# Cached keys of the sample attention: four loads by quarters of partitions and a 32 by 32 block transpose on VectorE, in place of one load, four TensorE transposes and a copy

## The chip, the cores and the metric

The kernel runs on one core of one Trainium2 chip. The metric is the device time of one execution in microseconds, the median of several runs. The engines that the text speaks of are TensorE (PE; its weight loads are PEld), VectorE (DVE), ScalarE (ACT), GpSimd (POOL) and SyncE (SP), whose instruction list holds the DMA issues. The transfers themselves run on the core's 16 DMA engines.

## The reference

One step of a hybrid layer is computed for two request groups that share all weights: a prompt of 2048 tokens, and 8 sample sequences of 16 tokens each that have a cache of 1024 keys and values. The model width is 1024.

```python
h = rms_norm(x, norm_g[l])
(a_x, a_b, a_c, a_z, g_q, g_f, g_i, g_z,
 s_q, s_k, s_v, s_z, m_a, m_b, m_c) = split_cols(h @ w_in[l])
...
y_conv, conv_new = causal_conv(a_c * a_x, conv_w[l], conv_past)   # branch A
...
S_new, o_hg = hgrn_scan(S0, q_hg, log_f, k_in, v_hg)              # branch B
...
q = rms_norm(s_q.reshape(B, T, SB_HEADS, SB_DH), q_norm_g[l])     # branch C
k = rms_norm(s_k.reshape(B, T, SB_HEADS, SB_DH), k_norm_g[l])
v = s_v.reshape(B, T, SB_HEADS, SB_DH)
if past_k is None:
    o_sb = sb_prompt(q, k, v)
else:
    o_sb = sb_attend(q, concat([past_k, k]), concat([past_v, v]), P + jnp.arange(T), jnp.arange(P + T))
...
m = sigmoid(m_a) * y_a + sigmoid(m_b) * y_b + sigmoid(m_c) * y_c
return x + m @ w_out[l], conv_new, S_new, k, v
```

The change lies in the last case of branch C, the attention of the 8 sample sequences over their caches. Its scores are `z = q k / 8` per head; for each query the weights are `sigmoid(z)` times the product of `sigmoid(-z)` over all later keys, and the result is their sum over the values. There are 8 heads of 64. The cached keys lie in memory as (sequence, key, head, 64), in float32, so a key's 8 heads are a row of 512 numbers, 2 KB. For the scores the 64 numbers of a head must lie along the partitions, so the keys have to be turned.

## The kernel before, in words

**Stages.** The tokens are 17 tiles of 128, tile 0 being the samples. They go through the input projection in three groups (`GROUPS`, L39) of 5, 6 and 6 tiles; then come the rest of the prompt attention and the merge with the output projection. In each group `run_jobs` (L1317 on) walks a list of jobs. A job is one block of weights and what is done with its product: a channel job (`proj_chan`, L704 to 714) holds 24 matmuls of 128x384 for each of two chunks of three tiles (L710), a token job (`proj_tok`, L716 to 725) 72 matmuls of 128x256 for each (L721). Each product is made in three passes of a high and a low half (`PASS3`), and `split` (L173 to 176) makes the halves: ScalarE copies the high half, VectorE subtracts it for the low one.

**Weights.** In the first group weights are read from `w_in` and split, and the halves are kept in device memory (`W<-w`). In later groups `wload` (L188 to 219) reads the kept halves: mostly both in one load of 1 MB (`w<-W`, L208), every fourth time in two loads of 512 KB (`wst<-W`, L201). Weights of job i+1 are loaded when job i starts; the pool has three buffers for `w` and two for `wst`.

**Background work.** `sample_attention` (L389 on) is a generator. It is added after the first group, and between the matmuls of the jobs of group 1 `run_jobs` lets it go on, at a rate that `RATES` and the yielded costs set (L1365); what is left is drained at the group's end (L1381). All of it lies between about 560 and 1340 us of the profiled execution. A scheduler then puts each engine's instructions into an order of its own, by its own costs, so that the order in the code is not the one that runs. DMAs are issued by SP in that order; one that waits for its producer or its buffer holds up all behind it.

**The step that is changed.** The cache has 8 blocks of 128 keys for each of 8 sequences, 64 blocks in all. They are handled in 24 groups of 2 or 3 blocks. `keys(m)` (L448 to 461) handles the blocks of group m. For each block it loads 128 keys with all heads into `kc`, 128 partitions of 2 KB (L455, 256 KB); has TensorE make four transposes of 128x128 with the unit matrix `idf` into PSUM (L458); and has ScalarE copy the result to the turned keys `kt` (L459). `kc` has three buffers, `kt` two. `scores` (L470 to 491) multiplies the queries with `kt` on TensorE (L476), takes two sigmoids on ScalarE and a scan and a product on VectorE (L489, L490). `turned` (L493 to 511) turns the weights (L499) and loads the values (`vc`, L506), and `values` (L513 to 530) multiplies them (L522) and stores the rows (L529).

**Other names.** `GM<-gm` (L1177) stores a merge gate after each chunk of a gate job, `SZ<-gm` (L1185) a SiLU gate. `OX<-...` (L182) stores branch results in two halves. `mwx`, `mwp` (L1298, L1302) are loads, splits and stores of the merge weights, spread over group 1. `post_qk` (L809 to 831) handles the normed queries and keys. `xt` are tiles of activations for the next group.

Of the kernel before, what the change touches and what calls it, by code (L numbers as in the profile page):

```python
# [8 lines left out]
F32 = mybir.dt.float32  # L9
# [7 lines left out]
P = 128  # L17
# [81 lines left out]
def trunk(ctx: ExitStack, tc: tile.TileContext, x_prompt, x_sample, cache_conv, state_hgrn, cache_k, cache_v,  # L99
# [3 lines left out]
    nc = tc.nc  # L103
# [37 lines left out]
    def ps_tp(dt=F32):  # L141
        return pst[0].tile([P, 512], dt, tag="tp", name="tp")
# [19 lines left out]
    idf = const.tile([P, P], F32, name="idf")  # L162
# [226 lines left out]
    def sample_attention():  # L389

        sx = ExitStack()
        sa = sx.enter_context(tc.tile_pool(name="sa", bufs=2, side="right"))
# [52 lines left out]
        def blocks(m):  # L445
            return 2 if order[m][1] == 2 else 3

        def keys(m):  # L448

            b, sg = order[m]  # L450
            kt = sa.tile([P, 4, 384], F32, tag="kt", name="kt", bufs=2)
            for bi in range(blocks(m)):
                blk = 3 * sg + bi
                kc = sa.tile([P, 512], F32, tag="cst", name="kc", bufs=3)
                nc.sync.dma_start(kc, cache_k[0, b, blk * P:(blk + 1) * P].rearrange("t h d -> t (h d)"))  # L455
                tp = ps_tp()
                for h in range(4):
                    nc.tensor.transpose(tp[:, h * P:(h + 1) * P], kc[:, h * P:(h + 1) * P], idf)  # L458
                nc.scalar.copy(kt[:, :, bi * P:(bi + 1) * P], tp.rearrange("p (h t) -> p h t", h=4))  # L459
                yield 1.3  # L460
            held[m] = [kt]

# [69 lines left out]

        last = len(order) - 1
        yield from keys(0)
        scores(0, masked(0))
        yield 0.7
        for m in range(last + 1):
            if m < last:
                yield from keys(m + 1)
            turned(m)  # L540
            yield 2.0
            z = masked(m + 1) if m < last else None
            values(m)
            if z is not None:
                scores(m + 1, z)
            yield 2.2
        oc = sa.tile([P, 512], F32, tag="cst", name="oc", bufs=3)
        nc.sync.dma_start(oc, OCS)
        tp = ps_tp()
# [982 lines left out]
```

## Time and profile before

| | us |
|---|---|
| median of 3 runs | 2872.75 (2871.84 to 2873.47) |
| profiled execution, its own time | 2876.11 |
| its span, first to last instruction | 2873.2 |
| TensorE busy in the span | 2853.0 |
| VectorE / ScalarE / GpSimd busy | 1546.5 / 1018.7 / 331.8 |
| 64 key blocks: loads issued | 563.2 to 1119.0 |
| 64 key blocks: transposes on TensorE | 599.1 to 1138.6 |

The profile is one execution of the program. Matmuls are pipelined, so that the time of one (its "mean ns") holds an overlap with its neighbours; what a matmul adds to the path is read from the chain of waits. The windows view gives each engine's busy time in a stretch of the span, the clock granted to TensorE, the share of the 16 DMA engines in use and what they moved. A row of the waits view is: engine, tile and line that waited, what it waited for, us in total, times, longest. "To landing" is the time from a DMA's issue to the landing of its data. SPq is SP's own queue of instructions.

### The profile page before, as it was taken

How to read it: one execution, taken by the hardware profiler on the slowest of the kernel's cores; microseconds unless marked ns; L12 is line 12 of the kernel's file. 1: busy time of each engine (PE TensorE's matmuls, PEld its weight loads, DVE VectorE, ACT ScalarE, POOL GpSimd, SP SyncE). 2: the span in 40 equal slices, each digit the busy share in tenths (PEclk: the TensorE clock that was granted, in tenths of full speed). 3: DMA queues.
4: the chain of work that ended last, by engine and by line, in shares of the span. 5: the costliest groups of instructions: out<-in, count | busy, mean ns of one | idle time of the engine just before them, and what ended most of it. 6: DMA issues, size and time to landing. Idle time of an engine off the chain costs nothing.

```text
span 2873.2 us, 51723 instructions
## 1 busy us (share of the span) xinstructions
PE 2853.0 (99%) x19479; PEld 2662.3 (93%) x19479; DVE 1546.5 (54%) x3304; ACT 1018.7 (35%) x2375; POOL 331.8 (12%) x802
## 2 busy tenths in 40 slices
PE   9999999999999999999999999999999999999999
PEld 9999999999999999999999999999998888787888
DVE  5454635641344442545434747557485876867743
ACT  4333222242233332213334444434444444544420
POOL 3110000111200000001323111111010011010100
PEclk9999999999999999999999999999999999999999
DMA  8887777777678887746766454544447877878876
GB/s 306 305 276 247 231 241 244 231 243 243 212 249 266 276 265 243 243 167 192 237 215 202 146 173 136 173 139 151 144 145 238 286 234 239 266 250 266 271 250 210
DMA packets 370475, 649.76 MB, mean 226 GB/s; under 512 B 33481, under 2 KB 246306, under 8 KB 339506
## 3 DMA queue, kind: packets, MB, share of 16 engines
q1 hardware_dynamic: 369458, 644.36, 68.2%
q8 instruction: 154, 2.52, 0.4%
q0 software_dynamic: 768, 2.10, 0.2%
q14 instruction: 95, 0.78, 0.1%
HBM read 447.06 MB, written 199.27 MB: 225 GB/s over the span
## 4 chain that ended last, share of the span: by engine, by line
PE 76%; DVE 2%; DMA 2%; issue 1%; ACT 0%; POOL 0%; SPq 0%; DVEq 0%; POOLq 0%; ACTq 0%
PE acc L710 33%; PE acc L721 10%; PE acc L1440 9%; PE acc L1471 6%; PE pv L359 4%; PE tp L310 4%; PE z L330 2%; PE z L329 2%; PE z L1039 1%; PE tp L458 1%; DMA gate<-GM 1%; PE pv L522 1%; PE z L476 0%; PE hg L1086 0%; PE hg L826 0%
## 5 line engine op out<-in xcount | busy, mean ns | idle before, releaser
L710 PE MATMUL acc<-hx,w 128*128 128x384 f32 (+1 forms) x6816 | 1251.8, 333 | 0.1
L710 PEld LDWEIGHTS acc<-hx,w 128*128 128x128 f32 x6816 | 1106.5, 188 | 21.9 <-issue 15.2
L721 PE MATMUL acc<-w,hx 128*128 128x256 f32 x2544 | 328.6, 284 | 1.8 <-DVE hx L176 0.9
L342 DVE TENSOR_TENSOR_SCAN pr<-snb,carry 128x513 f32<-128x513 f32 x192 | 246.5, 1284 | 153.3 <-ACT snb L333 151.7
L721 PEld LDWEIGHTS acc<-w,hx 128*128 128x128 f32 x2544 | 310.9, 188 | 5.0 <-DVE hx L176 1.7
L311 ACT COPY aT<-tp 128x512 f32<-128x512 f32 (+2 forms) x320 | 167.6, 524 | 375.2 <-PE tp L310 361.3
L710 PE MATMUL acc<-hx,wst 128*128 128x384 f32 x1248 | 247.2, 344 | 0.0
L1440 PE MATMUL acc<-o,w 128*128 128x512 f32 (+2 forms) x1080 | 234.7, 363 | 1.8 <-DMA o<-OX 1.8
L333 ACT ACTIVATE snb<-z 128x512 f32<-128x512 f32 (+2 forms) x320 | 172.4, 539 | 144.5 <-PE z L330 140.4
L710 PEld LDWEIGHTS acc<-hx,wst 128*128 128x128 f32 x1248 | 215.4, 188 | 6.4 <-issue 3.7
L1440 PEld LDWEIGHTS acc<-o,w 128*128 128x128 f32 x1080 | 185.1, 188 | 33.8 <-issue 5.3
L347 DVE TENSOR_TENSOR sp<-sp,pr 128x512 f32<-128x512 f32 (+2 forms) x320 | 195.3, 611 | 29.2 <-POOL sp L338 3.7
L342 DVE TENSOR_TENSOR_SCAN pr<-snb,one 128x129 f32<-128x129 f32 (+3 forms) x128 | 114.4, 894 | 123.9 <-POOL snb L338 123.6
L310 PE MATMUL tp<-idf,sp 128*128 128x128 f32 x1088 | 171.3, 273 | 2.5 <-ACT aT L311 1.5
L335 ACT ACTIVATE sp<-z 128x512 f32<-128x512 f32 (+2 forms) x320 | 171.5, 536 | 0.0
L1471 PE MATMUL acc<-w,mh 128*128 128x256 f32 x816 | 161.2, 285 | 1.0 <-DVE yt L1479 0.8
L1176 ACT ACTIVATE gm<-acc 128x384 f32<-128x384 f32 (+1 forms) x144 | 68.2, 474 | 230.4 <-PE acc L710 197.5
L310 PEld LDWEIGHTS tp<-idf,sp 128*128 128x128 f32 x1088 | 131.8, 141 | 19.3 <-issue 4.4
L176 DVE TENSOR_TENSOR w<-wst,w 128x1024 fp32r<-128x1024 f32 x72 | 88.1, 1223 | 110.7 <-ACT w L175 107.9
L1471 PEld LDWEIGHTS acc<-w,mh 128*128 128x128 f32 x816 | 131.0, 188 | 7.2 <-issue 4.2
L329 PE MATMUL z<-Kt,Q 128*128 128x512 f32 (+2 forms) x320 | 128.8, 403 | 0.3 <-ACT sp L335 0.2
L359 PE MATMUL pv<-aT,Vt 128*64 128x512 f32 (+3 forms) x640 | 128.1, 535 | 0.0
(299 smaller groups left out, 3570.1 us busy)
## 6 DMA issues: line engine op xcount, KB each, us to landing
w<-W SPq DMA_DIRECT2D x168, 1024.0 KB, 6.0
W<-w SPq DMA_DIRECT2D x72, 1024.0 KB, 5.0
wst<-W SPq DMA_DIRECT2D x112, 512.0 KB, 5.1
wst<-in_w_in_dram SPq DMA_DIRECT2D x72, 512.0 KB, 5.1
GM<-gm SPq DMA_DIRECT2D x120, 192.0 KB, 3.7
W<-mwp SPq DMA_DIRECT2D x40, 512.0 KB, 4.2
Kt<-KT SPq DMA_DIRECT2D x160, 128.0 KB, 3.1
o<-OX SPq DMA_DIRECT2D x72, 256.0 KB, 4.7
```

Source lines behind the costliest of these rows:

```text
L310: nc.tensor.transpose(tp[:, j * P:(j + 1) * P], sp[:, j * P:(j + 1) * P], idf)
L311: nc.scalar.copy(aT[:, e, 0:nb, i * P:(i + 1) * P], tp[:, :w].rearrange("p (b q) -> p b q", q=P))
L329: nc.tensor.matmul(z[:, :w], Q1[:, i * P:(i + 1) * P], Kt[:, :w], start=True, stop=False)
L333: nc.scalar.activation(sn[:, 512 - w:512], z[:, :w], AF.Sigmoid, scale=-0.125)
L335: nc.scalar.activation(sp[:, :w], z[:, :w], AF.Sigmoid, scale=0.125)
L342: nc.vector.tensor_tensor_scan(pr[:, 512 - w:513][:, ::-1], s_in, s_in, one if diag else carry[e][i], ALU.mult, ALU.bypass)
L347: nc.vector.tensor_tensor(sp[:, :w], sp[:, :w], pr[:, 513 - w:513], ALU.mult)
L359: nc.tensor.matmul(pv[64 * e:64 * e + 64, c0:n], Vt[:, j, e], aT[:, e, j, c0:n], start=first and j == 0, stop=last and j == nb - 1, skip_g ...
L710: nc.tensor.matmul(acc[:, :n], w[0][a][:, k], hT[b][:, k, :n], start=k == 0 and i == 0, stop=k == KB - 1 and i == 2)
L721: nc.tensor.matmul(acc[:, :256], hT[b][:, k, ti * P:(ti + 1) * P], w[k // 4][a][:, k % 4], start=k == 0 and i == 0, stop=k == KB - 1 and i ...
L1440: nc.tensor.matmul(acc[:, :n], w[0][a][:, k, dd * P:(dd + 1) * P], box[x][b][:, k, sl], start=k == 0 and i == 0, stop=k == 3 and i == 2)
L1471: nc.tensor.matmul(acc[:, :256], box["l" if b else "h"][:, k, ti * P:(ti + 1) * P], w[k // 4][a][:, k % 4], start=k == 0 and i == 0, stop= ...
```

## The change

Only `keys(m)` is changed. `kc` becomes a tile of `[128, 4, 4, 32]`, the same bytes with the same three buffers. It is filled by four DMAs. The `a`-th of them fills partitions 32a to 32a+31: partition 32a+p gets, for each of four pairs of heads h and each of four groups c of 32 keys, the numbers 32a to 32a+31 of key 32c+p. Each DMA so moves 64 KB in 512 runs of 128 bytes. Then one `transpose` on VectorE, which turns each block of 32 by 32 in place, writes the block of `kt`. TensorE's four transposes, the PSUM tile and ScalarE's copy go. `kt` holds the same numbers as before. Lines behind the change have numbers one higher.

```diff
             for bi in range(blocks(m)):
                 blk = 3 * sg + bi
-                kc = sa.tile([P, 512], F32, tag="cst", name="kc", bufs=3)
-                nc.sync.dma_start(kc, cache_k[0, b, blk * P:(blk + 1) * P].rearrange("t h d -> t (h d)"))
-                tp = ps_tp()
-                for h in range(4):
-                    nc.tensor.transpose(tp[:, h * P:(h + 1) * P], kc[:, h * P:(h + 1) * P], idf)
-                nc.scalar.copy(kt[:, :, bi * P:(bi + 1) * P], tp.rearrange("p (h t) -> p h t", h=4))
+
+                kc = sa.tile([P, 4, 4, 32], F32, tag="cst", name="kc", bufs=3)
+                keys_ = cache_k[0, b, blk * P:(blk + 1) * P].rearrange("(c p) h d -> p c (h d)", p=32)
+                keys_ = keys_.rearrange("p c (h x) -> p h c x", x=P)
+                for a in range(4):
+                    nc.sync.dma_start(kc[32 * a:32 * a + 32], keys_[:, :, :, 32 * a:32 * a + 32])
+                nc.vector.transpose(kt[:, :, bi * P:(bi + 1) * P].rearrange("p h (c q) -> p h c q", q=32), kc)
                 yield 1.3
```

The scheduler orders all engines anew. Two places of the resulting order are shown.

The first is SP's list in the middle of group 1, around the load of a kept weight, `W_3188`. Before, it stands between two key loads; behind it come stores of branch results (`OX`), merge weights (`W_9533`, `mwx`) and the next weights (`wst`):

```order
L455 DMA kc<-in_cache_k_dram 128x512
L208 DMA w<-W_3188 128x2048
L455 DMA kc<-in_cache_k_dram 128x512
L506 DMA vc<-in_cache_v_dram 128x512
L455 DMA kc<-in_cache_k_dram 128x512
L182 DMA OX<-sg 128x384
L182 DMA OX<-y 128x384
L1298 DMA W_9533<-mwp 256x1x512
L1302 DMA mwx<-in_w_branch_dram 128x2x256
L201 DMA wst<-W_3264 128x1024 x2
L182 DMA OX<-sg 128x384
L182 DMA OX<-y 128x384
```

Directly behind these, still before the change, come the first two gate stores (`GM<-gm`):

```order
L506 DMA vc<-in_cache_v_dram 128x512 x2
L509 DMA vnew<-VV 16x512
L1177 DMA GM<-gm 128x384
L182 DMA OX<-oh 128x256
L1298 DMA W_9533<-mwp 256x1x512
L182 DMA OX<-ob 128x256
L1302 DMA mwx<-in_w_branch_dram 128x2x256
L208 DMA w<-W_3327 128x2048
L1177 DMA GM<-gm 128x384
```

After the change the same weight stands here in SP's list (a key block is now four rows in one, `x4`; `oh` and `ob` are the two halves of a branch result):

```order
L182 DMA OX<-sg 128x384
L182 DMA OX<-y 128x384
L208 DMA w<-W_3083 128x2048
L1299 DMA W_9497<-mwp 256x1x512
L1303 DMA mwx<-in_w_branch_dram 128x2x256
L182 DMA OX<-oh 128x256
L182 DMA OX<-ob 128x256
L1178 DMA GM<-gm 128x384
L459 DMA kc<-in_cache_k_dram 32x16x32 x4
L1178 DMA GM<-gm 128x384
L208 DMA w<-W_3188 128x2048
```

So the load of `W_3188` has moved from ahead of both pairs of `OX` stores to directly behind the second gate store.

The second place is TensorE's list in the same part of group 1. Before, two blocks of key transposes (`tp<-idf,kc`) stand among the matmuls of channel jobs, ahead of a transpose of attention weights (`tp<-idf,sps`):

```order
L710 MATMUL acc<-hx,w 128x384 x18
L1112 MATMUL tp<-idf,on 128x128 x2
L710 MATMUL acc<-hx,w 128x384 x6
L458 MATMUL tp<-idf,kc 128x128 x4
L710 MATMUL acc<-hx,w 128x384 x6
L710 MATMUL acc<-hx,wst 128x384 x6
L458 MATMUL tp<-idf,kc 128x128 x4
L710 MATMUL acc<-hx,wst 128x384 x18
L499 MATMUL tp<-idf,sps_7051 128x128 x3
```

After it, the key transposes are gone and the matmuls of the jobs close up; the scores (`z<-kt,qz`) read what VectorE has turned:

```order
L1113 MATMUL tp<-idf,on 128x128 x2
L711 MATMUL acc<-hx,w 128x384 x48
L477 MATMUL z<-kt,qz 32x384
L523 MATMUL pv<-vc,at__10632 32x128 x12
L477 MATMUL z<-kt,qz 32x384 x3
L468 LDWEIGHTS idb
L468 MATMUL z<-nmask,idb 128x16
L711 MATMUL acc<-hx,wst 128x384 x4
L500 MATMUL tp<-idf,sps_7051 128x128 x3
```

Outside the stretch from about 560 to 1340 us TensorE's order is the same but for small exchanges.

## Prediction

> **What bounds the kernel now.** I read the page's busy times first, then the windows view by stages, then TensorE's waits in the stage of the change, then the chain of waits there. "Key stage" below is 560 to 1150 us: the cached keys are loaded and turned in it and nowhere else.
>
> From the page, the span and the busy times:
> ```profile
> span 2873.2 us, 51723 instructions
> PE 2853.0 (99%) x19479; PEld 2662.3 (93%) x19479; DVE 1546.5 (54%) x3304; ACT 1018.7 (35%) x2375; POOL 331.8 (12%) x802
> ```
> From the windows view, the opening of the kernel (0 to 100, 0 to 200) and the key stage:
> ```profile
> core 0: us, PE busy (x) PEld busy (x) DVE busy (x) ACT busy (x) POOL busy (x), PEclk, DMA share, GB/s
> 0.00:100.00 100.00, 96.13 (x722) 93.70 (x723) 50.15 (x96) 43.95 (x84) 29.96 (x81) 1.00 0.90 311
> ...
> 0.00:200.00 200.00, 195.84 (x1486) 192.94 (x1487) 91.86 (x189) 79.56 (x164) 45.11 (x104) 1.00 0.88 299
> ...
> 560.00:1150.00 590.00, 587.23 (x4588) 566.38 (x4587) 226.15 (x587) 187.50 (x469) 52.38 (x92) 1.00 0.76 250
> ```
> From the waits view of the key stage, all of TensorE's:
> ```profile
> PE tp L1112 <- DVE hx L176: 1.4, 1, 1.4
> PE tp L458 <- DVE hx L176: 0.8, 1, 0.8
> PE tp L1112 <- ACT on L1108: 0.6, 1, 0.6
> ```
> From the chain of waits of the key stage, its shares by line:
> ```profile
> by line: PE acc L710 56.0%; PE acc L721 23.2%; PE tp L458 4.8%; PE pv L522 3.1%; PE z L476 2.4%; PE z L1039 2.1%; PE tp L499 1.3%; PE hg L826 0.9%; DMA xt<-in_x_prompt_dram 0.7%; PE hg L1086 0.5%; PE tp L1088 0.5%; PE hg L1084 0.5%; PE z L1
> ```
> TensorE is busy 587 of the 590 us, at clock 1.00, and waits 2.8 us. So the stage ends when TensorE is through its list, and the chain is its matmuls, the key transposes (L458) among them. ScalarE (188) and VectorE (226 of 590) have room. The DMA engines stand at 0.76: not the bound, but the next thing to it.
>
> The execution that these rows come from took 2876.1 us, 2.9 around its span and 3.4 above the median of the three runs, 2872.75. Differences are worked out inside its span and taken from that median.
>
> **The change, part by part.**
>
> *Off TensorE: 256 transposes; off ScalarE: 64 copies.* Groups of the key stage, and two pieces of its chain:
> ```profile
> L458 PE MATMUL tp<-idf,kc 128*128 128x128 f32 x256 | 38.5, 273 | 0.8 <-DVE hx L176 0.8
> L459 ACT COPY kt<-tp 128x512 f32<-128x512 f32 x64 | 37.5, 588 | 58.6 <-PE tp L458 58.3
> ```
> ```profile
> 746.98 0.44 PE tp L458 x4
> ...
> 766.05 0.44 PE tp L458 x4
> ```
> 273 ns is the time of one transpose with its overlap; on the path four take 0.44 us, 110 ns each. 256 x 0.11 = **28.2 us**, which is also the chain's 4.8% of 590. This comes off the path. The 37.5 us of copies lie on an engine busy a third of the time; ScalarE appears in no wait of TensorE worth a microsecond, so they count for nothing.
>
> *Onto VectorE: 64 block transposes of 128x512.* No such operation is in the trace. Nearest rows: the multiply and the scan on tiles of that size.
> ```profile
> L347 DVE TENSOR_TENSOR sp<-sp,pr 128x512 f32<-128x512 f32 (+2 forms) x320 | 195.3, 611 | 29.2 <-POOL sp L338 3.7
> L342 DVE TENSOR_TENSOR_SCAN pr<-snb,carry 128x513 f32<-128x513 f32 x192 | 246.5, 1284 | 153.3 <-ACT snb L333 151.7
> ```
> So 39 to 82 us; I take 0.61 us, since one pass over one input is nearer a multiply than a serial scan. VectorE would be busy 265 (at most 308) of 590: hidden. Where a transpose reaches VectorE before its keys have landed, everything behind it on that engine waits, the low half of the next activations among it. TensorE's own waits on VectorE are two now (2.2 us); I price this at 0, with up to 5 us for the range.
>
> *Onto SP's queue: 256 issues for 64.* Issues of many short runs in the SP rows of the timeline:
> ```profile
> 884.04 0.52 SPq L1298 DMA_DIRECT2D W<-mwp  x1
> ...
> 885.26 0.82 SPq L1302 DMA_DIRECT2D mwx<-in_w_branch_dram  x1
> ```
> 192 more at 0.33 (a key load's shortest now) to 0.6 us are 63 to 115 us of a queue that spends far more of the stage waiting for producers. The price is not the issuing but what it stands in front of, below.
>
> *Onto the DMA engines: the same 16.8 MB in 131,072 runs of 128 bytes instead of 8,192 of 2 KB.* From the DMA view, 560 to 1150 and then 0 to 200:
> ```profile
> DMA packets 78082, 147.57 MB, mean 250 GB/s; under 512 B 8834, under 2 KB 43906, under 8 KB 72374
> ```
> ```profile
> DMA packets 46772, 59.87 MB, mean 299 GB/s; under 512 B 2737, under 2 KB 42178, under 8 KB 43410
> ```
> In the key stage a full share moves 250/0.76 = 329 GB/s, so the keys now cost 16.8 MB/329 = 51 us of all 16 engines, out of 0.76 x 590 = 448. In the opening a full share moves 299/0.88 = 340 GB/s, 21 bytes per ns and engine, while most packets are short (weight columns in rows of 512 bytes and 1 KB). At that rate 128 bytes take 6 ns and a 512-byte row 24; a run of 128 bytes lies between, and I take the middle, **15 ns**. Then the keys cost 131,072 x 15/16 = 123 us (49 at 6 ns, 197 at 24), and the stage's DMA work is 448 - 51 + 123 = 520 us (446 to 594). Over a stage of 578 that is a share of 0.90, the highest that the rows show, and there 520/0.90 = 578 is just what the stage would take if DMA set it.
>
> The Trainium skill ("DMA: Bandwidth & Descriptors", section "Why small descriptors are slow (HBM only)") puts a fixed 3 cycles on each packet beside one per 32 bytes. By that a key load would cost (16 x 7)/67 = 1.67 times its present price, an estimate from that page: 85 us instead of 51, a share near 0.84, landings near 7.3, and the sum below nearer -22. No run here shows that price yet.
>
> *Moved: the weight loads.* The order of the queue is made anew, and SP's weight loads now stand behind stores that wait for their producers. Four rows and the landing times carry it: the issue of W_3188 before (SP), the second gate store after it (SP), the first matmul that uses W_3188 (PE), and how long such a load takes.
> ```profile
> 864.30 0.49 SPq L208 DMA_DIRECT2D w<-W  x1
> ...
> 887.28 0.32 SPq L1177 DMA_DIRECT2D GM<-gm  x1
> ```
> ```profile
> 898.12 1.31 PE L710 MATMUL acc<-hx,w 128*128 128x384 f32 x6
> ```
> ```profile
> L208 SPq DMA_DIRECT2D w<-W x168: 319/338/1574, 570.5 to 2845.6; - x168
> ...
> DMA to landing us min/median/max: 4.7/6.0/8.8
> ```
> Before, W_3188 is issued 33.8 us ahead of its use. In the new order it stands directly behind that second gate store, so it goes no sooner than 887.6: 10.5 us ahead, less 0.9 for the two blocks of transposes that no longer lie between. W_4031 is the worst that I found: behind a gate store, ahead of a use at
> ```profile
> 923.49 0.37 SPq L1177 DMA_DIRECT2D GM<-gm  x1
> ```
> ```profile
> 930.66 1.12 PE L710 MATMUL acc<-hx,w 128*128 128x384 f32 x5
> ```
> that is 6.8 us. I put each of the 65 weight DMAs between 600 and 1150 against the last store ahead of it in the new order, at that store's time before: 30 have 10.5 us or less, 15 of them 6.7 to 9, some 7.9 in the middle. A load takes 6.0; behind two or three blocks of keys, each 2,048 x 15/16 = 1.9 us of the engines instead of 0.8, it takes 6.0 + 2.5 x 1.1 = 8.8. So 15 loads are late by 0.9 us: **14 us**, on the path, because TensorE has nothing else in its list there. Ends: 0 (landing stays at 6.0 and beats every lead) and 40 (all 30 late by 1.3). The start of the stage already loses
> ```profile
> 590.65 4.34 DMA xt<-in_x_prompt_dram
> ```
> to a late load of activations; the first keys' runs go beside it. I add **1.5 us** for that (0 to 4).
>
> Sum: -28.2 + 14 + 1.5 = -12.7 us. Against the profiled execution that is 2863.4; against the median **2860**.
>
> **The rivals.**
>
> *B, the full gain.* Landings stay near 6 us and every weight is in time: -28.2, so 2844.6. For it: the shortest lead, 6.8 us, is above the median landing, and the pools let SP slip ahead when TensorE slips. Against: the largest landing, 8.8, is above 15 leads already.
>
> *D, nothing gained.* The work taken away becomes waiting: weights late at 30 places by about 0.9 us, or VectorE's queue held by transposes whose keys are late, so that activations come late. 28 lost, 2872.75. For it: the leads; TensorE never waited for weights in this stage before, so there was nothing to show how such a wait grows.
>
> *C, slower: the DMA engines become the bound.* The stage then takes its DMA work over the share reached, (397 + 131,072 t/16,000)/0.90 us with t in ns per run. It equals 590 at t = 16.4, so that is the point from which it decides. At 18 ns the stage takes 605, +15, 2888; at 24 ns 660, +70, 2943. For it: 0.76 already, break-even hardly above my 15, and a share that swings in the DMA view's slices of the stage (in tenths), so that a mean of 0.90 may not be reached:
> ```profile
> DMA  8877396976773946798778877989775969894795
> ```
> Against: at 6 to 13 ns it costs nothing. The Trainium skill has a rule against the change here ("DMA: Bandwidth & Descriptors", section "Specifications"): below 512 bytes a transfer misses the line rate, because the engine reads, modifies and writes. By it rival C is the likelier; no trace of before shows a price for that.
>
> That the change would not do what it says has no place: the transposes and the copies are gone from the order.
>
> **How the numbers follow.** Partial gain, the forecast (-6 to -22, so 2851 to 2867): 0.44, for it follows from terms that are each near the middle. B: 0.13. D, within 0.2%, which is 5.7 us and about what a measurement of this kernel can tell from no change: 0.13. C: 0.30, as 15 and 16.4 ns lie close together in a span of 6 to 24. Faster 0.44 + 0.13 = 0.57, same 0.13, slower 0.30. The range goes from the full gain and a little, 2843, to C at some 18 ns, 2890; it leaves out about half of C and a scrap of B, under 0.2.
>
> **What would show it.** Right: the rows of L458 and the copy gone, the block transpose near 0.6 us in VectorE's groups, the DMA share of the key stage near 0.90, weights landing in 8 to 9 us, and TensorE's waits naming weight DMAs for 10 to 20 us in a stage of about 577. B: share below 0.85, no such waits. C: share at 0.9 or above over the whole stage, landings of 10 us and more, TensorE waiting for weights and keys by more than 28 us. D: TensorE's waits near 28, or naming VectorE's kt or hx. The forecast is wrong in its first term if a transpose on the path was worth less than 110 ns; in its second if the waits lie elsewhere than at the weights.

## The result, and the profile after

| | us | ratio to before, 95% interval |
|---|---|---|
| before, median of 4 runs | 2873.11 | |
| after, median of 4 runs | 2994.6 (2990.45 to 2996.97) | 1.0419 [1.0401, 1.0437] |

The change makes the kernel 121 us slower; 2860 was forecast, with 2890 as the upper end. The profiled execution has a span of 2991.0 us, 117.8 more than before.

The page of the kernel after, its busy times, TensorE's clock and the DMA share by slices, and its main DMA queue:
```profile
span 2991.0 us, 51341 instructions
PE 2886.3 (96%) x19223; PEld 2659.1 (89%) x19223; DVE 1586.1 (53%) x3368; ACT 983.3 (33%) x2311; POOL 333.4 (11%) x802
...
PEclk9999999999999898999999999999999999999999
DMA  9887777768668677685677545453535886877876
...
q1 hardware_dynamic: 495410, 644.37, 67.7%
```
The transposes are gone, and TensorE is nevertheless busy 33 us longer; outside its busy time it idles 2991.0 - 2886.3 = 104.7 us, where it idled 20.2. The DMA engines did not fill up.

The windows view of the stages, and the worst 100 us:
```profile
560.00:1150.00 590.00, 522.94 (x3659) 478.30 (x3658) 227.85 (x568) 128.09 (x345) 46.50 (x79) 0.94 0.69 198
1150.00:1340.00 190.00, 168.37 (x1125) 154.34 (x1124) 71.67 (x191) 39.25 (x103) 7.02 (x12) 0.96 0.79 237
900.00:1000.00 100.00, 79.65 (x495) 70.56 (x495) 28.63 (x66) 17.72 (x42) 0.89 (x2) 0.85 0.81 230
```
In 590 us TensorE got through 3659 matmuls instead of 4588, of which 256 were the key transposes. From 560 to 1340 it idles 780 - 522.9 - 168.4 = 88.7 us, and its granted clock is 0.94 and 0.96, 0.85 in the worst part, where it had been 1.00 all along. The DMA share of the key stage is 0.69, below the 0.76 of before.

TensorE's waits from 560 to 1340, the largest, and VectorE's largest:
```profile
PE z L477 <- DVE kt L460: 26.3, 7, 8.8
PE tp L500 <- DVE sps L491: 11.7, 10, 2.8
PE acc L711 <- DMA wst<-W: 10.7, 5, 4.7
PE tp L1113 <- ACT on L1109: 10.1, 5, 2.6
PE acc L711 <- DMA w<-W: 9.9, 3, 4.9
PE z L1040 <- DVE WL L1035: 5.8, 7, 1.0
```
```profile
DVE kt L460 <- DMA kc<-in_cache_k_dram: 83.3, 14, 18.4
```
The waits are not for one thing. Weights (20.6 us) are a part; the turned keys, the attention's products and the recurrence's tiles come late as well. Behind the turned keys stands VectorE, which waits 83 us for loads of keys.

The key loads and the block transposes (min, median and max in ns; first and last start):
```profile
L459 SPq DMA_DIRECT2D kc<-in_cache_k_dram x256: 578/635/3088, 561.8 to 1256.7; - x128
L460 DVE STREAM_TRANSPOSE kt<-kc x64: 668/704/715, 578.6 to 1270.5; 128x512 f32<-128x512 f32 x64
```
The last load goes at 1256.7, before at 1119.0: the background work has been stretched over 138 us more.

How such a stretch looks, from the chain of waits between 880 and 910 us:
```profile
888.13 0.28 ACT od L528
888.43 0.32 SPq L530
...
892.03 0.60 SPq L459
892.68 0.64 SPq L459
893.36 0.63 SPq L459
894.03 0.64 SPq L459
894.67 0.04 issue
894.72 6.75 DMA w<-W
```
SP stores a sequence's result as soon as ScalarE has it (eight stores, L530), issues four quarters of a block, and only then the weights that TensorE needs next, which land 6.75 us later. That is a chain that runs through SP's list, and TensorE stands at its end: its next matmuls start at 901.51, when the weights are there.

### The profile page after: what moved, and what is told of

It is laid out like the page before. It is cut to its first block, busy times and chain, and to the rows that moved or that the text cites. A ratio compares the mean times of both kernels' runs of the same rounds, so it can differ in the third digit from the quotient of the medians.

```text
span 2991.0 us, 51341 instructions
## 1 busy us (share of the span) xinstructions
PE 2886.3 (96%) x19223; PEld 2659.1 (89%) x19223; DVE 1586.1 (53%) x3368; ACT 983.3 (33%) x2311; POOL 333.4 (11%) x802
## 3 DMA queue, kind: packets, MB, share of 16 engines
q1 hardware_dynamic: 495410, 644.37, 67.7%
## 4 chain that ended last, share of the span: by engine, by line
PE 89%; DVE 3%; DMA 3%; SPq 2%; issue 1%; ACT 1%; POOL 1%; another core or an unknown queue 0%; DVEq 0%; ACTq 0%; POOLq 0%
PE acc L711 41%; PE acc L722 12%; PE acc L1441 9%; PE acc L1472 7%; PE pv L359 4%; PE tp L310 4%; PE z L330 2%; PE z L329 2%; PE z L1040 2%; SPq L459 1%; DMA wst<-W 1%; DMA w<-W 1%; SPq L530 1%; PE pv L523 1%; PE z L477 1%
## 5 line engine op out<-in xcount | busy, mean ns | idle before, releaser
L711 PEld LDWEIGHTS acc<-hx,w 128*128 128x128 f32 x6816 | 1125.0, 191 | 34.5 <-issue 26.2
L711 PEld LDWEIGHTS acc<-hx,wst 128*128 128x128 f32 x1248 | 222.0, 193 | 18.7 <-issue 12.0
L1177 ACT ACTIVATE gm<-acc 128x384 f32<-128x384 f32 (+1 forms) x144 | 68.2, 474 | 271.8 <-PE acc L711 230.3
```

What stands on the lines that cost most here:

```text
L711: nc.tensor.matmul(acc[:, :n], w[0][a][:, k], hT[b][:, k, :n], start=k == 0 and i == 0, stop=k == KB - 1 and i == 2)
```

## Experiments

My first theory was SP's occupation: 256 issues of 0.64 us make everything behind them late. The rivals were the short runs, VectorE's list, and the order as such. Ratios are to the kernel before in the same batch; a ratio's hundredth of a per cent is 0.29 us. Where long loads meet VectorE's transpose, where quarters meet TensorE's, and in one_short, the keys end in the wrong places; those kernels serve to measure time only.

| kernel | loads of a block, queue | turned by | order | us | ratio [95%] |
|---|---|---|---|---|---|
| one_long | 1 of 2 KB rows, SP | VectorE | own | 2847.8 | 0.9911 [0.9894, 0.9928] |
| one_short | 1 of 128-byte runs, SP | VectorE | own | 2861.08 | 0.9959 [0.9945, 0.9973] |
| four_long | 4 of 2 KB rows, SP | VectorE | own | 2905.07 | 1.0107 [1.0090, 1.0124] |
| four_short_pe | quarters, SP | TensorE | own | 3006.4 | 1.0455 [1.0438, 1.0473] |
| extra_brief | 1 long + 3 of 32 runs, SP | VectorE | own, the same for both | 2865.01 | 0.9970 [0.9960, 0.9980] |
| extra_many | 1 long + 3 of 512 runs, SP | VectorE | own, the same for both | 2881.72 | 1.0029 [1.0018, 1.0040] |
| quarters_pool | quarters, GpSimd | VectorE | own | 2871.43 | 0.9984 [0.9973, 0.9994] |
| quarters_act | quarters, ScalarE | VectorE | own | 2894.53 | 1.0080 [1.0059, 1.0102] |
| quarters_by_group | quarters of 2 or 3 blocks, SP | VectorE | own | 2992.3 | 1.0406 [1.0389, 1.0424] |
| group_on_pool | the same, GpSimd | VectorE | own | 2869.11 | 0.9979 [0.9970, 0.9989] |
| weights_sooner | quarters, SP | VectorE | own | 2989.66 | 1.0403 [1.0386, 1.0421] |
| weights_on_pool | quarters, SP | VectorE | own | 2945.78 | 1.0245 [1.0228, 1.0262] |
| change_old_order | quarters, SP | VectorE | one_long's | 2926.28 | 1.0184 [1.0168, 1.0200] |
| long_new_order | 1 of 2 KB rows, SP | VectorE | the change's | 2965.41 | 1.0320 [1.0306, 1.0334] |
| quarters_before_order | quarters, SP | TensorE | before's | 2911.83 | 1.0133 [1.0118, 1.0149] |

### Which part of the change costs

**one_long**: the transpose alone.
```diff
-                for a in range(4):
-                    nc.sync.dma_start(kc[32 * a:32 * a + 32], keys_[:, :, :, 32 * a:32 * a + 32])
+                src = cache_k[0, b, blk * P:(blk + 1) * P].rearrange("t h d -> t (h d)")
+                nc.sync.dma_start(kc.rearrange("p h c q -> p (h c q)"), src)
```


> One load of 128 rows of 2 KB per block, as before the change, with the block transpose on VectorE kept; the turned keys are then in the wrong places, so the sample attention's numbers are left wrong. Theory of SP's queue (the 256 issues of 0.64 us and more make everything behind them late): the loads are the old ones, so the full gain of the forecast comes, 28 us, about 2845. Rival, VectorE's list (a transpose that waits for its keys holds up the low halves and the attention's products behind it) or the new order as such: still clearly slower than before, 2920 or more, with TensorE waiting for kt and sps.

2847.8, 0.9911 of before: 26 us (21 to 30) gained. Its block transposes take as long as in the change, its clock is 1.00, and TensorE is as busy in the key stage as before:
```profile
L458 DVE STREAM_TRANSPOSE kt<-kc x64: 674/702/714, 564.6 to 1085.6; 128x512 f32<-128x512 f32 x64
```
```profile
560.00:1150.00 590.00, 587.01 (x4520) 566.38 (x4519) 281.48 (x712) 159.47 (x424) 52.09 (x92) 1.00 0.78 259
```
Turning on VectorE costs nothing that shows and gives what the first term of the forecast said. VectorE's list as a cause by itself is out.

**one_short**: as many short runs, in one issue.
```diff
+                src = cache_k[0, b].rearrange("(p r) h d -> p (r h d)", r=8)[:, 2048 * (blk % 2):2048 * (blk % 2) + 2048]
+                src = src.rearrange("p (n x) -> p n x", x=P)[:, :, 32 * (blk // 2):32 * (blk // 2) + 32]
+                nc.sync.dma_start(kc.rearrange("p h c x -> p (h c) x"), src)
```


> One load per block, but of 128 partitions with 16 runs of 128 bytes each (2,048 runs, the same number of runs and bytes as in the change, from other places of the cache, so the sample attention's numbers are wrong), with VectorE's transpose. Theory of SP's queue, if an issue costs by the instruction: 64 issues, 2845 to 2865. Theory of SP's queue, if an issue costs by the runs in it: each issue takes some 2.5 us, and the time is that of the change, about 2990. Theory of short runs (the DMA engines or the landing are what is slow): about 2990 with issues below 1 us.

2861.08: 13 us above one_long. Its 64 issues take 78 us in all, against 31 in one_long. The same number of runs of 128 bytes brings the DMA share to 0.87 in the key stage and does no great harm there:
```profile
560.00:1150.00 590.00, 580.92 (x4448) 556.56 (x4447) 275.08 (x678) 157.16 (x417) 54.16 (x94) 1.00 0.87 252
```

**four_long**: four issues per block, without short runs.
```diff
+                for a in range(4):
+                    nc.sync.dma_start(kc[32 * a:32 * a + 32].rearrange("p h c q -> p (h c q)"), src[32 * a:32 * a + 32])
```


> Four loads per block, each of 32 partitions with one row of 2 KB, with VectorE's transpose (the turned keys are in the wrong places, so the sample attention's numbers are wrong). Theory of SP's queue, by the instruction: four issues at 0.33 us and up, about 90 us of issues more than before, 2900 to 2990. Theory of SP's queue, by the runs: 32 runs each, short issues, 2850 to 2880. Theory of short runs: 2850 to 2865.

2905.07, 57 us above one_long: four issues hurt more than short runs, and this spoke for SP's queue. The two together (57 + 13) still are half of what the change lost against one_long (147 us by the medians, 146 by the ratios). Each of these kernels has an order of its own, so its loss holds what that order costs as well.

**four_short_pe**: the quarter loads with the old way of turning.
```diff
-                nc.vector.transpose(kt[:, :, bi * P:(bi + 1) * P].rearrange("p h (c q) -> p h c q", q=32), kc)
+                tp = ps_tp()
+                for h in range(4):
+                    nc.tensor.transpose(tp[:, h * P:(h + 1) * P], kc[:, h].rearrange("p c q -> p (c q)"), idf)
+                nc.scalar.copy(kt[:, :, bi * P:(bi + 1) * P], tp.rearrange("p (h t) -> p h t", h=4))
```


> The four loads of the change with TensorE's four transposes and ScalarE's copy as before the change (what is turned is then laid out wrongly, so the sample attention's numbers are wrong). Theory of SP's queue and theory of short runs: as slow as the change and about 28 us more for the transposes, 2990 to 3020. Rival, VectorE's list: the loss goes with the transposes on VectorE, so 2875 to 2890.

3006.4: the loads, with the order that the scheduler makes for them, make the loss, whoever turns the keys.

### Is it SP?

**quarters_pool** and **quarters_act**: the same loads from another engine.
```diff
-                    nc.sync.dma_start(kc[32 * a:32 * a + 32], keys_[:, :, :, 32 * a:32 * a + 32])
+                    nc.gpsimd.dma_start(kc[32 * a:32 * a + 32], keys_[:, :, :, 32 * a:32 * a + 32])
```


> The change with its 256 quarter loads issued from GpSimd's queue instead of SP's; the same bytes and runs, and nothing else is altered. SP's queue then holds 64 DMAs less than before the change. Theory of SP's queue: the loss goes, and what is left is the price of the short runs, as one load of short runs showed it: 2855 to 2875. Rival, too many DMAs at once (the number of transfers in flight, or short runs by quarters being slow in themselves, from whichever queue): near the change, 2950 or more.

> The change with its 256 quarter loads issued from ScalarE's queue instead of SP's. Theory of SP's queue: SP is free, but ScalarE now makes some 200 us of issues among the sigmoids and high halves, and each waits for a free key buffer; half of the loss goes, 2880 to 2940. If ScalarE has room for it: 2855 to 2880. Rival, transfers in flight: near the change, 2950 or more.

2871.43 and 2894.53 (there with `nc.scalar`). Off SP, 256 loads of the same bytes and runs cost 24 and 47 us against one_long, not 147, with the share at 0.86 and 0.84. Neither the DMA engines nor many transfers in flight can be the main cause.

**quarters_by_group** and **group_on_pool**: fewer and larger issues, straight into `kt`.
```diff
+            for a in range(4):
+                nc.sync.dma_start(kc[32 * a:32 * a + 32], src[:, :, :, 32 * a:32 * a + 32])
+            for bi in range(n):
+                part = kc[:, :, 4 * bi:4 * bi + 4]
+                nc.vector.transpose(part, part)
+                yield 1.3
```


> Quarter loads on SP, but for a whole group of two or three blocks in one (96 issues for 256), straight into the tile of turned keys, which VectorE then turns in place; the same bytes in the same 131,072 runs of 128 bytes. Theory of SP's queue, by the instruction: 96 issues at 0.65 us are 62 us against some 200, little more than the loads before the change took; 2850 to 2880. By the runs: three times 0.65 each, near the change, 2950 to 2990.

> Quarter loads for a whole group (96 in all), straight into the tile of turned keys and turned in place, issued from GpSimd. If what made the loads by group as slow as the change was their place on SP: 2855 to 2875. If it was the turning in place with two buffers, which lets the next group's load start only when the scores are through: 2950 to 2990.

2992.3 on SP, with 96 issues in place of 256. That was against my theory. The issues became longer, but their sum fell: 96 with a mean of 1.26 us are 121 us, against 203 us for the 256 of the change. The same loads from GpSimd: 2869.11. That pair moves both SP's time and the place of the loads, and each kernel has its own order, so it does not part the two by itself. The traces do more: from 560 to 1340 us all of SP's issues together take 370 us in quarters_by_group and 404 us in one_short, and the first loses 144 us against one_long, the second 13. The time that SP spends on issues does not set the loss.

**weights_sooner**: the weights are asked for a job ahead.
```diff
             if g or at_:
                 weights(i + 1)
+            if g == 1 and ci and len(jobs[min(i + 2, n - 1)][0][0]) == len(jobs[min(i + 1, n - 1)][0][0]) == 1:
+                weights(i + 2)
```


> The change with the weights of the group asked for one job sooner where the three buffers allow it (single-piece jobs); the key loads are untouched. Theory of the forecast (the weights stand too late in SP's order, and TensorE waits for them): the 22 us of weight waits go and with them most of what follows, 2900 to 2960. Theory of SP's queue (SP is full, and whatever is put sooner makes something else later): within 20 us of the change, 2975 to 3010.

2989.66, 5 us below the change, which is not clear of the noise: asking sooner does not make them go sooner. The weights loaded between 560 and 1150 us are issued 11 us ahead of their job's first matmul on average, in the change 12.

**weights_on_pool**: weights of group 1 from GpSimd's queue; the two half loads (`wst`) are altered in the same way.
```diff
-                nc.sync.dma_start(w.bitcast(F32), kept[key, n].bitcast(F32))
+                (nc.gpsimd if stage[0] == 1 else nc.sync).dma_start(w.bitcast(F32), kept[key, n].bitcast(F32))
```


> The change with the kept weights of group 1 loaded from GpSimd's queue, so that they stand behind nothing of SP's; the quarter loads stay on SP. If late weights are what costs: 2870 to 2900. If SP's lateness reaches TensorE by the keys and stores as well: 2920 to 2970, with waits for kt left. If neither (transfers in flight, the DMA engines): 2980 or more.

2945.78: 49 us of the loss go when the weights stand behind nothing of SP's, and 98 against one_long stay. The lists of the other engines changed with it, so the 49 us are not the weights' alone.

**extra_brief** and **extra_many**: one long load, and three idle loads more per block, in one and the same order.
```diff
+                for a in range(3):
+                    nc.sync.dma_start(dm[32 * a:32 * a + 32], src[32 * a:32 * a + 32, 0:4])
```


> The kernel with one long load per block and the transpose on VectorE, and three more loads per block on SP, each of 32 partitions with one run of 16 bytes, into a tile that nobody reads (256 key-related issues as in the change, next to no bytes; the sample attention's numbers are wrong as in that kernel). The scheduler gives this kernel and the next one the same order, in which weights stand a few stores later than with one load. Theory of occupancy (SP is late because issues take long): 192 issues at 0.33 us are 63 us spread over the stage, 2848 to 2865. Theory of the order (each DMA more on SP moves weights behind stores that wait for their producers, whatever an issue takes): 2890 to 2940, and the same as the next kernel within 15 us.

> As the kernel with three brief extra loads, but each extra load has 16 runs of 4 bytes in each of 32 partitions, 512 runs as in a quarter load, with next to no bytes. Same order of all instructions. Theory of occupancy: 192 issues at 0.6 us and more, about 120 us, 2890 to 2950 and 30 us or more above the kernel with brief loads. Theory of the order: within 15 us of that kernel.

2865.01 and 2881.72. The first row is of the brief loads, the second of those with 512 runs (there `keys_[:, :, :, 32 * a:32 * a + 1]`):
```profile
L460 SPq DMA_DIRECT2D dm<-in_cache_k_dram x192: 311/421/1181, 561.8 to 1132.0; - x192
```
```profile
L462 SPq DMA_DIRECT2D dm<-in_cache_k_dram x192: 578/635/1929, 562.4 to 1148.9; - x192
```
The second has the very issue time of a quarter load, 635 ns, and costs 17 us more than the first and 34 more than none. With that SP's occupation by loads that gate nothing has a price: 17 us within one order and at most 34, not 147. Both theories missed in part: extra_brief stands at the upper edge of occupancy's range, and extra_many is 17 us above it, between the two forecasts. Far below 2890, the two also show that more entries on SP do not make the bad order by their number alone.

### The order against the loads

What was left was the order that the scheduler makes. These three kernels pin it: when the program is complete, each instruction is told to be queued behind another one on its engine, for all five engines, after a list taken from another kernel.
```diff
+        for a, b in zip(order, order[1:]):
+            tc.add_manual_dep(by[b], a, mybir.DependencyInfo(mybir.DependencyClass.NoSync,
+                                                             mybir.DependencyReason.DATA), reason="order")
```


> The change as it is, four quarter loads per block on SP and the transpose on VectorE, but with every engine's list pinned to the order that the scheduler gave the kernel with one long load; each block's four loads stand one behind the other where the one load stood. Theory of the order (the scheduler, to which 256 loads on SP look dear, puts weights, keys and stores of all engines later, and the chip then waits for what the list puts late): the loss goes, 2855 to 2885, the price of the issues and of the short runs left. Theory of occupancy (SP really is that slow): 2940 or more, in whatever order.

> One long load per block and the transpose on VectorE, as in the first experiment, but with every engine's list pinned to the order of the change; each load stands where the last of the four quarters stood (the sample attention's numbers are wrong, as there). Theory of the order: slow in spite of cheap loads, 2920 to 2985. Theory of occupancy: as with one long load in its own order, 2845 to 2870.

> The kernel before with its loads alone changed to quarters (TensorE's transposes and ScalarE's copies stay; what is turned is laid out wrongly, so the sample attention's numbers are wrong), and every engine's list pinned to the order of the kernel before. In its own order this kernel took 3006. Theory of the order: 2880 to 2910. Theory of occupancy: 2970 or more.

2926.28, 2965.41 and 2911.83. The second lies in the order's range; the first fell between the two forecasts, the third 2 us above the order's. In the traces every engine's list is that of its model, entry for entry with a block's quarters taken as one. Before 560 and after 1340 us a pinned kernel keeps step with its model to within 2 us (long_new_order to within 4), so the pins cost next to nothing there. In us against the kernel before (the ratio less one, times 2874):

| | long loads | quarter loads |
|---|---|---|
| one_long's order | -26 | +53 |
| the change's order | +92 | +120 |

Against one_long, cheap loads in the change's order lose 118 us; the change's loads in the good order lose 79 instead of 146. Both halves of the theories hold, the order's the larger, and they overlap: both together lose 146, not their sum of 197. With TensorE's transposes it is alike: quarter loads in the order of before lose 38 us, in their own order 131.

The windows of long_new_order show the picture of the change again, idle TensorE and a lower clock, with the DMA engines at 0.63:
```profile
560.00:1150.00 590.00, 536.31 (x3793) 490.34 (x3793) 234.76 (x579) 132.96 (x355) 46.68 (x79) 0.96 0.63 212
```
TensorE's waits there from 560 to 1340 us, the larger ones:
```profile
PE z L475 <- DVE kt L458: 18.2, 8, 4.0
PE tp L498 <- DVE sps L489: 11.3, 10, 2.8
PE tp L1111 <- ACT on L1107: 10.1, 5, 2.6
PE z L1038 <- DVE WL L1033: 6.2, 9, 1.0
PE acc L709 <- DMA wst<-W: 2.9, 1, 2.9
PE acc L709 <- DMA w<-W: 2.7, 2, 1.4
```
They are those of the change, but for fewer waits for weights. And its chain shows how an order can do it, with no slow transfer in it (the weights' 6.88 us compare with a median of 6.6 in the key stage before; 952 to 971 us; what is left out is the rest of the eight stores, two more loads of keys and two gate stores):
```profile
954.47 0.40 PE pv L521 x8
...
954.89 0.28 ACT od L526
...
955.18 0.32 SPq L528
...
958.85 0.52 SPq L1297
...
959.41 1.40 SPq L1301
...
960.85 0.51 SPq L457
...
963.43 6.88 DMA w<-W
...
970.44 1.62 PE acc L709 x4
```
The keys of the next group (L457) and the weights (L208) stand behind the stores of this sequence's result, which wait for `od`. VectorE's list has reached the transpose by then:
```profile
965.07 0.71 DVE L458 STREAM_TRANSPOSE kt<-kc 128x512 f32<-128x512 f32 x1 [12.43 <-DMA kc<-in_cache_k_dram]
```
It stands there for 12.4 us, and with it the low halves that are next in its list, `mwp` first, which other entries of SP wait for. Here each list waits for the next one around a circle: TensorE for weights and keys, SP for products of ScalarE and VectorE, VectorE for keys. Put each weight load against the first matmul of its job, and the mean time between the two, for loads issued from 560 to 1150 us, is 26 us in one_long and 25 in change_old_order, 13 in long_new_order and 12 in the change: lateness of the weights comes with the order, not with the loads. It is 19 us in extra_brief and extra_many, and 26 in quarters_pool and group_on_pool, where the keys are off SP.

In the good order the quarters leave the weights alone; this is all that TensorE waits for them in change_old_order from 560 to 1340 us:
```profile
PE acc L711 <- DMA w<-W: 1.0, 1, 1.0
```
The lateness seems to sit in the keys. VectorE's wait for them in the same time, first in one_long, then in change_old_order:
```profile
DVE kt L458 <- DMA kc<-in_cache_k_dram: 22.8, 7, 9.7
```
```profile
DVE kt L460 <- DMA kc<-in_cache_k_dram: 75.7, 26, 10.9
```
That the loads cost 38 us with TensorE's transposes and 79 with VectorE's fits that; it was not tried by itself, since orders differ in the two. VectorE's wait is no price by itself: quarters_act has 92.0 us of it and is 32 us faster than change_old_order.

## Why the prediction was wrong

- **Transposes off TensorE, 28.2 us: right.** one_long gained 26 [21, 30].
- **Transposes on VectorE: right in size, 0.70 us instead of 0.61, and hidden as such.** "I price this at 0, with up to 5 us for the range" for transposes that reach VectorE ahead of their keys was wrong: 83 us of waiting on VectorE, and 26 us of TensorE's waits name `kt`. With the loads and order of one_long the price of 0 held.
- **The DMA engines: right in the price of a run, not in the share.** q1 took 67.7% of 2991.0 us of the 16 engines, 2025 us, and 68.2% of 2873.2, 1960, before. The 65 us more with the 51 of before are 116 for the keys, 14.2 ns a run where 15 was taken. In quarters_act, where the keys have a queue to themselves, it is 3.8% of 2889.9 us, 110. The rule on small packets that the Trainium skill has ("DMA: Bandwidth & Descriptors", section "Why small descriptors are slow (HBM only)") gave 85 us by the prediction's estimate; the trace says 116, 2.3 times the old price and not 1.67. The share of 0.90 that was to follow did not come, and rival C fell: the share was 0.69 in the change, and where it did reach 0.87, in one_short, the loss was 13 us.
- **SP's issues: too small.** The 63 to 115 us more were 172: 203 us instead of 31. "The price is not the issuing but what it stands in front of" was right in the main, but not wholly: 192 issues of that length that gate nothing cost up to 34 us.
- **The moved weight loads: the failed step.** "So 15 loads are late by 0.9 us: 14 us", with 40 as the upper end. The leads were near the truth: 30 of 65 loads at 10.5 us or less were forecast, and of the 51 issued from 600 to 1150 us 27 were, 21 of them at 9 or less. The sum over them was not. The landing of 6.0 us was the median of the whole kernel; in the key stage it was 6.6, which alone would have made 14 us some 22. The large error is another: I held every store at the time that it had before, and counted each late load once, as if the next began on time. In a list of which each entry waits for another engine's list, lateness is passed on. By the order alone 118 us were lost (long_new_order). From 560 to 1340 us TensorE idles 64 us there against 5 in one_long; waits for weights are 5.6 us of that, and `kt`, `sps` and other tiles are named for most of the rest. weights_on_pool points the same way: with the weights off SP, 98 us of 147 stay.
- **The clock, not in the sum at all.** The mean granted clock fell from 1.000 to 0.985. On 2991 us that is 45 us. With the 84 us more of idle time it makes 129 of the 146 us that were lost beside the 28 gained; the other 17, of TensorE's longer busy time, stay unexplained. The trace's record of the clock shows more than the mean. In the kernel after it is at half in 15 stretches between 590 and 1236 us, each of 3.41 us or up to five times that, 89 us together. In the kernel before and in one_long there is none. Three windows of 3.41 us: the one before such a stretch, the stretch, and one at full clock:
```profile
825.67:829.08 3.41, 1.44 (x7) 1.16 (x8) 1.44 (x3) 0.00 (x0) 0.00 (x0) 1.00 0.78 295
829.08:832.49 3.41, 3.41 (x13) 3.41 (x12) 0.29 (x1) 0.62 (x1) 0.00 (x0) 0.50 0.88 183
846.15:849.56 3.41, 3.41 (x21) 3.41 (x20) 0.14 (x1) 0.29 (x1) 0.00 (x0) 1.00 0.69 147
```
  At half, 13 matmuls of 128x384 fill the time that 21 fill at full clock. The Trainium skill states this rule ("TensorE: Matmul & The Clock Gate", section 'Part 1: The HAM clock gate (the "warmup" mystery)'): TensorE's clock is halved after a window of some 3.4 us without work. The trace agrees on the halving and on the 3.41 us, but not on the window without work: TensorE was busy for 1.44 of the 3.41 us before the stretch shown, and before all 15 it had idled for 1.1 to 3.4 us of the window, only once for the whole of it. So waits shorter than the window cost clock too.

Rival D had the mechanism in its words (weights late, VectorE's queue held by transposes without keys) and gave it 28 us, because that was the time set free; the runs show 118 us of it by the order alone. Its sign, waits that name `kt`, came true. The chance of 0.30 for slower was put on the DMA engines alone, and they were not the cause.

What stays open: why the scheduler's order for the quarters is so much worse, which of its entries cost how much, how the 79 us of the quarters in the good order divide between SP and VectorE, and why group_on_pool gains only 6 of the 28 us, when by one_short the short runs cost 13.

## What to carry to other kernels

When a change multiplies the entries of an in-order queue that other engines wait behind, price the new order and not only the new entries: pin the old order on the new kernel, and the new order on the old one, and the two causes come apart. A change that frees 28 us on the bounding engine can lose five times that if it makes the lists wait for each other in a circle, and in these traces the clock falls where TensorE idles: from 560 to 1340 us it is 1.00 with 5 us idle (one_long), 0.96 with 56 (change_old_order) and 0.94 with 89 (the change). Here the quarter loads belong on another queue than SP's: issued from GpSimd by group they give 0.9979 [0.9970, 0.9989] of the time before, 6 us less. Of the kernels that leave nothing out, this one and quarters_pool (0.9984) are faster than before and after alike.

## What the runs showed of the hardware

- An issue on SP took 311 ns at least and 421 in the median for 32 partitions with one run, 578 and 635 for 32 partitions with 16 runs, whatever the bytes (4 or 128 a run). It doesn't go by the number of runs alone: one issue of 128 partitions with 16 runs took 370 at least, 624 in the median and 6.1 us at most (1.2 us in the mean).
```profile
L458 SPq DMA_DIRECT2D kc<-in_cache_k_dram x64: 370/624/6137, 563.0 to 1121.9; - x64
```
- 64 block transposes of 128x512 in float32 take 0.70 us each; four TensorE transposes of the same data took 0.44 us on the path.
- TensorE's granted clock was 0.85 over 100 us in which it was busy 80% of the time. It is a mean of full and half clock. Cut into windows of 3.41 us where the clock can change, the 17 traces show this: after a window at full clock in which TensorE idled for less than 1.0 us by the profile's busy times, the clock was never halved (7102 windows); after one with more than 2.0 us idle it always was (84).
